# A two-layer hybrid encoder on one core: q and k prepared for two token tiles at a time, large products taken off GpSimd, and the last steps of A's second unit moved behind the gate of C

## The chip, the cores and the metric

The kernel runs on one core of a Trainium2 chip. The number that counts is the device time in microseconds. The engines are TensorE (PE, with its weight load PEld), VectorE (DVE), ScalarE (ACT), GpSimd (POOL) and SyncE (SP, which here issues every DMA).

## The reference, cut to what matters

The input is 512 tokens of 1024 channels. Two layers follow each other; every layer normalises x, modulates it (scale, shift and gate come from a conditioning vector), multiplies it with one wide `w_in`, runs three mixers, multiplies their joined outputs with `w_out` and adds the gated result to x.

```python
for l in range(DEPTH):                                   # 2 layers
    shift, scale, gate = jnp.split(cs @ w_ada[l] + b_ada[l], 3, axis=-1)
    h = rms_norm(x, norm_g[l]) * (1.0 + scale[:, None]) + shift[:, None]
    qa, ka, va, ga, qb, kb, vb, gb, qc, kc, vc, gc = jnp.split(h @ w_in[l], split_idx, axis=-1)
    qa = rope(rms_norm(qa, qn_a[l]), ROT_THETA, ROT_A)   # A: 4 heads, two 32-wide maps each
    ka = rope(rms_norm(ka, kn_a[l]), ROT_THETA, ROT_A)
    oa = diff_attention(qa, ka, va, lam, ...)            # softmax1 - lam * softmax2, then rms_norm
    oa = oa * jax.nn.silu(ga)
    qb, kb = (rope(rms_norm(z, g), ROT_THETA, ROT_B) for z, g in ((qb, qn_b[l]), (kb, kn_b[l])))
    ob = dilated_attention(qb, kb, vb) * jax.nn.silu(gb) # B: 6 heads of 64
    qc, kc = (rope(z, RET_THETA, DK_C) for z in (qc, kc))
    oc = retention_bidir(qc, kc, vc, ret_decay[l], gn_c[l]) * jax.nn.silu(gc)   # C: 4 heads
    x = x + gate[:, None] * (jnp.concatenate([oa, ob, oc], axis=-1) @ w_out[l])
```

## The kernel before, in words

Tokens stand in four tiles of 128 (`NT`). Every weight is split into a rounded high part and a rest (`whi`, `wlo`), and so is the activation (`hT`, `hL`), so that each product of a layer is three matmuls (`products`, lines 342 to 348). The split costs ACT one copy (line 156) and DVE one subtraction (line 315) per piece of weights.

The columns of `w_in` come in chunks. Their order in a layer is: C's q, k and v; A's unit 0; B's unit 0; A's unit 1; B's units 1 and 2; the gate of C; the gate of B; then the output projection in two halves. Each chunk is 16 groups of matmuls (4 pieces of weights by 4 token tiles; the gate of B has 12). Everything that is not a product is hung on a plan: `at(g, fn)` runs `fn` right after group `g` is emitted, so the numbers at the top of the file say behind which group a step is written. A scheduler then sorts the instructions of each engine; each engine executes its own list strictly in that order. PE's list therefore holds, between the products of the next chunks, the attention work of the units before: scores (`sc`), transpositions (`tr`, four at a time, `tr4`, line 572, into a single buffer), values (`pv`).

What the change touches:

- `Unit`: a unit is two heads of q and k. `done` (per token tile) copies the tile's 256 columns of q and k from the accumulator to `qkraw` (a pool of four buffers). `norm` squares them on ACT into `qkn`, sums on DVE (line 625), finishes the mean on DVE (line 587) and takes the power -0.5 on POOL (line 199); it turns the rotary columns with two products and a sum (lines 633, 634, 635, all on DVE). `scale` multiplies by the result on POOL (line 639). `turn` transposes a pair of tiles on PE and writes the high and the low part (`nat`, ACT and DVE at line 159 for the low part); `stack` moves them with DMAs.
- `Attention.turn`: transposes the exponentials (`e` of A, `sb` of B) and copies them out of the transposition buffer on ACT or DVE (`pt`, line 708). `values` is the product with v.
- `Diff.finish` to `finish4`: the end of an A unit. `finish` copies the sums (`oat`); `finish2` transposes them, copies them (`oao`), squares them on POOL (`oasq`, line 765), sums (line 769); `finish3` scales (line 779) and multiplies by the gate on POOL (line 781); `finish4` transposes back and splits into `o`. `FIN2, FIN3, FIN4 = 4, 12, 16` say how many groups after the end of the attention they are written, for both units.
- `Retention.rope` (C's q and k): two products and a sum, of which two are on POOL (lines 913, 916). `Retention.gate_done` (lines 988 to 992) applies C's gate: `cth`, which also frees the accumulator bank. There are four banks.
- `out_done`: the residual sum is on POOL for the first half of the columns (line 1134).
- `Dilated.soft`: one reciprocal per head (line 813).

Buffers: `ep` is a ring of five tiles of 512 columns, tag `e`, from which scores, exponentials and many temporaries of all units come.

Of the kernel before, what the change touches and what calls it, by code (L numbers as in the profile page):

```python
# [48 lines left out]
E_T1, E_T2, E_X, E_QF, E_SCALE_A, E_SCALE_B = 1, 1, 1, 0, 0, 0  # L49
FIN2, FIN3, FIN4 = 4, 12, 16  # L50
# [84 lines left out]
def encoder(ctx, tc, x, c, norm_g, w_ada, b_ada, w_in, w_out, params, consts, out):  # L135
# [5 lines left out]
    four = pool("four", 4)  # L141
# [448 lines left out]
    class Unit:  # L590
# [6 lines left out]
        def done(self, t, ps, g0):  # L597
# [20 lines left out]
        def norm(self, t):  # L618
            n, ng_ = self.n, 256 // self.n
            rot, h = n // 4, n // 8  # L620
            raw = self.raw[t]
            qn = self.qn[t] = two.tile([P, ng_, n], F32, name="qkn", tag=f"qkn{t % 2}")
            act(qn.rearrange("p g n -> p (g n)"), raw, AF.Square)
            ss = self.ss[t] = sm.tile([P, 8], F32, name="qkss")[:, :ng_]
# [691 lines left out]
```

## Time and profile before

| | |
|---|---|
| time, three runs | 649.25, 651.51, 651.46 us, median 651.46 us |
| the profiled execution | 650.6 us, of which the span from first to last instruction is 648.7 us |
| PE busy | 622.2 us of the span |
| DVE busy | 491.8 us |
| ACT busy | 344.4 us |
| POOL busy | 163.7 us |

How to read it: busy is the union of an engine's instructions, so a PE that is busy nearly always leaves only the rest of the span to be won without changing the products. A line number belongs to the file before. In a group of instructions the mean is of one instruction; in a timeline an idle time in brackets stands before the instruction and names what ended it. Idle marks of PE are a little short, because a matmul's end is modelled and reaches beyond the start of the next one; the distance from start to start shows more.

### The profile page before, as it was taken

To read this page: it belongs to the slowest core of one execution; us is meant where nothing else is said; L and a number is where in the kernel's file an instruction comes from. 1 tells how busy PE (TensorE), PEld (TensorE's weight loads), DVE (VectorE), ACT (ScalarE), POOL (GpSimd) and SP (SyncE) were. 2 spreads that over 40 slices of the span, in tenths; PEclk is the share of its full clock that TensorE was granted. 3 is DMA by queue.
4 is the path that set the end of the run, shared out by engine and by line. 5 is a ranking of instruction groups with operands and counts; after the bars stand their busy time and mean duration, and the time that the engine had idled before them with its cause. 6 is when DMAs were issued, how large, how long until landed. Compare 5 with 4: busy or idle time off the path is not lost.

```text
span 648.7 us, 10469 instructions
## 1 busy us (share of the span) xinstructions
PE 622.2 (96%) x3487; PEld 512.2 (79%) x3487; DVE 491.8 (76%) x1206; ACT 344.4 (53%) x756; POOL 163.7 (25%) x183
## 2 busy tenths in 40 slices
PE   6899999999999996999999999999999999899997
PEld 1788888987888873677779998997788787677786
DVE  4787676689988987898969364768997997578443
ACT  4855263566646665564424344455756577566410
POOL 1105452514350510200411041633323340020000
PEclk9799999999999999999999999999999999999999
DMA  8998123535555556476643322235565453604211
GB/s 302 295 293 238 55 70 98 135 98 146 150 152 176 141 176 161 160 248 201 216 156 110 90 73 66 71 104 159 134 176 137 135 145 112 161 34 149 80 65 66
DMA packets 87277, 93.03 MB, mean 143 GB/s; under 512 B 7188, under 2 KB 68276, under 8 KB 87224
## 3 DMA queue, kind: packets, MB, share of 16 engines
q1 hardware_dynamic: 87224, 92.37, 48.0%
q8 instruction: 28, 0.46, 0.3%
q14 instruction: 25, 0.20, 0.1%
HBM read 72.42 MB, written 4.19 MB: 118 GB/s over the span
## 4 chain that ended last, share of the span: by engine, by line
PE 79%; DVE 9%; issue 4%; DMA 3%; POOL 3%; ACT 2%; SPq 1%; POOLq 0%; ACTq 0%
PE acc L346 16%; PE acc L348 16%; PE acc L347 16%; PE tr L572 8%; PE pv L718 5%; PE sc L741 2%; DMA x<-in_x_dram 2%; PE acc L344 1%; PE acc L342 1%; PE acc L343 1%; PE sc L802 1%; PE sc L803 1%; DVE wlo L315 1%; PE co L971 1%; DVE pt L708 1%
## 5 line engine op out<-in xcount | busy, mean ns | idle before, releaser
L346 PE MATMUL acc<-whi,hT 128*128 128x384 f32 (+1 forms) x424 | 154.7, 365 | 0.0
L347 PE MATMUL acc<-wlo,hT 128*128 128x384 f32 (+1 forms) x424 | 151.8, 358 | 0.0
L348 PE MATMUL acc<-whi,hL 128*128 128x384 f32 (+1 forms) x424 | 151.8, 358 | 0.0
L315 DVE TENSOR_TENSOR wlo<-raw,whi 128x384 fp32r<-128x384 f32 (+1 forms) x130 | 80.7, 650 | 26.7 <-ACT whi L156 26.4
L199 POOL TENSOR_TENSOR qkss<-qkss,nhalf 128x4 f32<-128x4 f32 (+1 forms) x40 | 52.6, 1315 | 128.3 <-DVE qkss L587 127.3
L346 PEld LDWEIGHTS acc<-whi,hT 128*128 128x128 f32 x424 | 80.0, 189 | 6.1
L348 PEld LDWEIGHTS acc<-whi,hL 128*128 128x128 f32 x424 | 79.8, 188 | 6.2
L347 PEld LDWEIGHTS acc<-wlo,hT 128*128 128x128 f32 x424 | 80.0, 189 | 5.5
L156 ACT ACTIVATE whi<-raw 128x768 fp32r<-128x768 f32 (+2 forms) x67 | 59.5, 890 | 39.7 <-PE acc L348 33.8
L159 DVE SCALAR_TENSOR_TENSOR ada_acc<-raw,cs,ada_acc 128x512 f32<-128x512 f32 x86 | 64.3, 749 | 3.9 <-DMA raw<-in_w_ada_dram 3.3
L156 ACT ACTIVATE e<-sc,mx 128x512 f32<-128x512 f32 x64 | 43.9, 689 | 35.5 <-DVE mx L743 16.9
L743 DVE TENSOR_REDUCE mx<-sc 128x1 f32<-128x512 f32 x64 | 43.5, 685 | 9.5 <-PE sc L741 8.8
L156 ACT ACTIVATE sb<-sb,mx 128x512 f32<-128x512 f32 x48 | 34.4, 717 | 20.4 <-DVE mx L807 20.2
L718 PE MATMUL pv<-pt,v 128*64 128x256 f32 x320 | 38.9, 385 | 1.0 <-DVE pt L708 0.9
L156 ACT ACTIVATE pt<-tr 128x512 f32<-128x512 f32 x40 | 23.8, 596 | 23.1 <-PE tr L572 22.9
L572 PE MATMUL tr<-cst,sb 128*128 128x128 f32 x192 | 30.7, 283 | 5.3 <-DVE nat L159 2.2
L807 DVE CUSTOM_DVE_ANT_0 sb<-sc,cst 128x512 f32<-128x512 f32 x48 | 32.1, 683 | 4.4 <-PE sc L803 2.6
L572 PEld LDWEIGHTS tr<-cst,sb 128*128 128x128 f32 x192 | 21.9, 142 | 16.0 <-ACT pt L156 7.7
L718 PEld LDWEIGHTS pv<-pt,v 128*64 128x64 f32 x320 | 21.2, 136 | 16.2 <-DVE pt L708 5.5
L708 DVE COPY pt<-tr 128x512 f32<-128x512 f32 x40 | 27.4, 684 | 7.8 <-PE tr L572 7.8
L639 POOL TENSOR_TENSOR qkn<-qkraw,qkss 128x256 f32<-128x256 f32 x40 | 30.0, 751 | 5.9 <-DVE qkraw L635 2.0
L741 PE MATMUL sc<-stk,stq 96*128 96x512 f32 x64 | 27.3, 434 | 1.0 <-ACT e L156 0.9
(294 smaller groups left out, 1367.8 us busy)
## 6 DMA issues: line engine op xcount, KB each, us to landing
raw<-in_w_ada_dram SPq DMA_DIRECT2D x64, 256.0 KB, 3.2
raw<-in_w_in_dram SPq DMA_DIRECT2D x48, 192.0 KB, 2.9
raw<-in_w_in_dram SPq DMA_DIRECT2D x24, 384.0 KB, 3.4
raw<-in_w_in_dram SPq DMA_DIRECT2D x32, 256.0 KB, 3.4
raw<-in_w_ada_dram SPq DMA_DIRECT2D x16, 512.0 KB, 5.1
raw<-in_w_out_dram SPq DMA_DIRECT2D x32, 256.0 KB, 3.0
x<-in_x_dram SPq DMA_DIRECT2D x8, 512.0 KB, 4.2
stB<-nat SPq DMA_DIRECT2D x32, 128.0 KB, 2.4
```

The source lines that it names most:

```text
L156: A.activation(o, i, f, **kw)
L159: V.scalar_tensor_tensor(o, a, s, b, op0, op1)
L199: G.tensor_tensor(o, i, nhalf[:, :n], OP.pow)
L315: V.tensor_tensor(l2[:, z], r2[:, z], h2[:, z].bitcast(F32), OP.subtract)
L346: T.matmul(ps, ah, hi[i], start=s_, stop=False)
L347: T.matmul(ps, ah, lo[i], start=False, stop=False)
L348: T.matmul(ps, al, hi[i], start=False, stop=e_)
L572: T.transpose(ps[:, i, :], b, ident)
L708: V.tensor_copy(pt, ps)
L718: T.matmul(self.pv[h * 64:h * 64 + 64, i * 256:i * 256 + 256], self.u.v[:, k, h * 64:h * 64 + 64], self.pt[h][:, k], start=k == 0, stop=k ...
L741: T.matmul(ps, self.u.stq[0:96, m, tok_(qt)], self.u.stk[0:96, m], start=True, stop=True)
L743: V.tensor_reduce(mx, ps, AX.X, OP.max, negate=True)
```

## The change

Four things are changed.

1. `norm` and `scale` work on a pair of token tiles (512 columns) instead of one (256). Each is called half as often, behind the second tile of the pair. `scale` is on DVE and is held in program order there. The pool `four` is gone: `qkraw` is now two buffers of a pair, and the gain loads `ng` and the tiles `hn` share the new sizes.
2. No large product is left on POOL: `scale`, the square of `finish2` (now on ACT), the gate product of `finish3`, two of the three steps of C's rotary turn and the residual sum of the first half are moved to DVE or ACT. POOL keeps the powers, the memsets and the rotary tables.
3. `FIN_A = (4, 12, 16), (14, 6, 9)`: unit 0 of A ends as before (4, then 12 and 16 after the first); unit 1 starts its `finish2` at 14 instead of 4, `finish3` at 20 instead of 16 and `finish4` at 23 instead of 20. `oat` and `oao` no longer take tiles of the ring `e`; they use the tiles in which the unit's output will stand, and `out_pair` is called in `finish4`.
4. `soft` takes one reciprocal for both heads.

```diff
-E_T1, E_T2, E_X, E_QF, E_SCALE_A, E_SCALE_B = 1, 1, 1, 0, 0, 0
-FIN2, FIN3, FIN4 = 4, 12, 16
+FIN_A = (4, 12, 16), (14, 6, 9)
-    four = pool("four", 4)
-        g = four.tile([P, 256], F32, name="ng", tag="qkraw")
+        g = two.tile([P, 256], F32, name="ng", tag="qkraw")
...
             g = g0 + 12 + t
-            at(g + NORM, self.norm, t)
-            at(g + SCALE, self.scale, t)
             if t % 2:
+                at(g + NORM, self.norm, t // 2)
+                at(g + SCALE, self.scale, t // 2)
                 at(g + TURN, self.turn, t // 2)
...
-        def norm(self, t):
-            n, ng_ = self.n, 256 // self.n
+        def norm(self, i):
+            n, ng_ = self.n, 512 // self.n
-            raw = self.raw[t]
-            qn = self.qn[t] = two.tile([P, ng_, n], F32, name="qkn", tag=f"qkn{t % 2}")
-            act(qn.rearrange("p g n -> p (g n)"), raw, AF.Square)
-            ss = self.ss[t] = sm.tile([P, 8], F32, name="qkss")[:, :ng_]
+            raw = self.raw[i].rearrange("p t (g n) -> p (t g) n", n=n)
+            qn = self.qn[i] = two.tile([P, ng_, n], F32, name="qkn")
+            act(qn, raw, AF.Square)
+            ss = self.ss[i] = sm.tile([P, 16], F32, name="qkss")[:, :ng_]
             V.tensor_reduce(ss, qn, AX.X, OP.add)
             rms_end(ss, ng_, n)
...
-        def scale(self, t):
-            n, ng_ = self.n, 256 // self.n
-            (V if (E_SCALE_A if n == DK_A else E_SCALE_B) % 2 else G).tensor_tensor(self.qn[t], self.raw[t].rearrange("p (g n) -> p g n", n=n),
-                            self.ss[t].unsqueeze(2).to_broadcast([P, ng_, n]), OP.mult)
+        def scale(self, i):
+            n, ng_ = self.n, 512 // self.n
+            tc.keep_in_program_order(V.tensor_tensor(self.qn[i], self.raw[i].rearrange("p t (g n) -> p (t g) n", n=n),
+                                                     self.ss[i].unsqueeze(2).to_broadcast([P, ng_, n]), OP.mult))
...
         def finish(self, g):
-            self.ob = ep.tile([P, S], F32, name="oat", tag="e")
+            self.ob = one.tile([P, S], F32, name="oat", tag=f"s{2 * self.k + 1}")
             act(self.ob, self.pv)
-            at(g + FIN2, self.finish2, g + FIN2)
+            at(g + self.fin[0], self.finish2, g + self.fin[0])
...
-            G.tensor_tensor(sq, o, o, OP.mult)
+            act(sq, o, AF.Square)
...
-            at(g + FIN3, self.finish3)
-            at(g + FIN4, self.finish4)
+            at(g + self.fin[1], self.finish3)
+            at(g + self.fin[2], self.finish4)
...
-            G.tensor_tensor(on, on, self.u.ga, OP.mult)
+            V.tensor_tensor(on, on, self.u.ga, OP.mult)
...
-            split(self.oh, self.ol, ps.rearrange("p t m -> p (t m)"))
+            split(*self.out_pair(self.k), ps.rearrange("p t m -> p (t m)"))
...
+            V.reciprocal(self.s, self.s)
             for h in range(2):
-                V.reciprocal(self.s[h], self.s[h])
...
-            G.tensor_tensor(t1.rearrange("p h (w n) -> p h w n", w=2), sw,
+            V.tensor_tensor(t1.rearrange("p h (w n) -> p h w n", w=2), sw,
...
-            G.tensor_tensor(self.qkp[:, :, :DK_C], raw, t1, OP.add)
+            V.tensor_tensor(self.qkp[:, :, :DK_C], raw, t1, OP.add)
...
-                    (V if hf * E_X % 2 else G).tensor_tensor(x_sb[t][:, cols], y, x_sb[t][:, cols], OP.add)
+                    V.tensor_tensor(x_sb[t][:, cols], y, x_sb[t][:, cols], OP.add)
```

How the instructions stand, at three places. In these rows a name carries its buffer's number; line numbers of the new file are two to six lower than those of the old one.

First place: PE in layer 0, where the products of C's gate have ended and those of B's gate (lines 342 to 344 before, 340 to 342 after) begin. `sb` are exponentials of B's units, `oat` the sums of A's unit 1. Before:

```order
L572 MATMUL tr_3033<-cst_103,sb_2932 128x128 x4
L802 MATMUL sc_3139<-stk_2907,stq_2906 128x512
L803 MATMUL sc_3139<-stk_2907,stq_2906 128x512
L572 MATMUL tr_3040<-cst_103,sb_2940 128x128 x4
L572 MATMUL tr_3047<-cst_103,oat_2926 128x128 x4
L572 MATMUL tr_3102<-cst_103,sb_2994 128x128 x4
L342 MATMUL acc_3175<-hT_118,whi_2977 128x512
L343 MATMUL acc_3175<-hL_119,whi_2977 128x512
L572 MATMUL tr_3108<-cst_103,sb_3002 128x128 x4
L344 MATMUL acc_3175<-hT_118,wlo_2978 128x512
L342 MATMUL acc_3175<-hT_118,whi_2977 128x512
L343 MATMUL acc_3175<-hL_119,whi_2977 128x512
```

After:

```order
L570 MATMUL tr_2882<-cst_100,sb_2786 128x128 x4
L800 MATMUL sc_2972<-stk_2760,stq_2759 128x512
L801 MATMUL sc_2972<-stk_2760,stq_2759 128x512
L340 MATMUL acc_3005<-hT_115,whi_2828 128x512
L341 MATMUL acc_3005<-hL_116,whi_2828 128x512
L570 MATMUL tr_2889<-cst_100,sb_2793 128x128 x4
L342 MATMUL acc_3005<-hT_115,wlo_2829 128x512
L340 MATMUL acc_3005<-hT_115,whi_2828 128x512
L341 MATMUL acc_3005<-hL_116,whi_2828 128x512
L342 MATMUL acc_3005<-hT_115,wlo_2829 128x512
L340 MATMUL acc_3038<-hT_115,whi_2828 128x512
L341 MATMUL acc_3038<-hL_116,whi_2828 128x512
```

The four transpositions of `oat` have left this place (they stand some 70 rows later, between products of B's gate), and the products of B's gate begin two transpositions earlier and stand between the others.

Second place: PE in layer 1, a little earlier in the layer, behind the second pair of q and k of B's unit 2 (`qkn`). Before, from the pair's last transposition on:

```order
L572 MATMUL tr_6424<-cst_103,qkn_6296 128x128
L347 MATMUL acc_6307<-wlo_6389,hT_118 128x384
L802 MATMUL sc_6512<-stB_6016,stC_6015 128x512
L803 MATMUL sc_6512<-stB_6016,stC_6015 128x512
L348 MATMUL acc_6307<-whi_6388,hL_119 128x384
L346 MATMUL acc_6333<-whi_6388,hT_118 128x384
L347 MATMUL acc_6333<-wlo_6389,hT_118 128x384
L348 MATMUL acc_6333<-whi_6388,hL_119 128x384
L346 MATMUL acc_6333<-whi_6388,hT_118 128x384
L347 MATMUL acc_6333<-wlo_6389,hT_118 128x384
```

After, from the transposition ahead of it to the next two:

```order
L570 MATMUL tr_6099<-cst_100,sb_5985 128x128 x4
L800 MATMUL sc_6202<-stB_5735,stC_5734 128x512
L801 MATMUL sc_6202<-stB_5735,stC_5734 128x512
L570 MATMUL tr_6115<-cst_100,qkn_5991 128x128 x4
L800 MATMUL sc_6209<-stB_5735,stC_5734 128x512
L801 MATMUL sc_6209<-stB_5735,stC_5734 128x512
L570 MATMUL tr_6170<-cst_100,sb_6060 128x128 x4
L570 MATMUL tr_6176<-cst_100,sb_6067 128x128 x4
```

Before, products stood between that pair and the next transposition (five more follow the rows shown); now a pair of score products is all that stands on either side of it.

Third place: DVE in the same stretch of layer 1, the work around the low parts `nat` of that pair. Before:

```order
L708 COPY pt_6413<-tr_6408 128x4x128
L807 ISA sb_6467,mx_6466<-sc_6463,cst_103 128x512
L807 ISA mx_6466 128x1
L813 RECIPROCAL bs_6461<-bs_6461 128x1
L159 SCALAR_TENSOR_TENSOR nat01_6349<-tr_6424,gcol_115,nat00_6348 128x256
L813 RECIPROCAL bs_6469<-bs_6469 128x1
L818 TENSOR_SCALAR sb_6467<-sb_6467,bs_6469 128x512
L159 SCALAR_TENSOR_TENSOR nat11_6351<-tr_6424,gcol_115,nat10_6350 128x256
L807 ISA sb_6516,mx_6515<-sc_6512,cst_103 128x512
L807 ISA mx_6515 128x1
L708 COPY pt_6413<-tr_6487 128x4x128
```

After:

```order
L705 COPY pt_6104<-tr_6099 128x4x128
L636 TENSOR_TENSOR qkn_5991<-qkraw_5934,qkss_5993 128x512
L809 RECIPROCAL bs_6146<-bs_6146 128x2
L805 ISA sb_6206,mx_6205<-sc_6202,cst_100 128x512
L805 ISA mx_6205 128x1
L815 TENSOR_SCALAR sb_6158<-sb_6158,bs_6146 128x512
L313 TENSOR_TENSOR wlo_6304<-raw_6259,whi_6303 128x384
L157 SCALAR_TENSOR_TENSOR nat01_6043<-tr_6115,gcol_112,nat00_6042 128x256
L313 TENSOR_TENSOR wlo_6304<-raw_6259,whi_6303 128x384
L157 SCALAR_TENSOR_TENSOR nat11_6045<-tr_6115,gcol_112,nat10_6044 128x256
```

The scaling of the pair (`qkn`) now stands in DVE's list between a copy `pt` and the low parts; before it was no instruction of DVE.

## Rows read from the trace of the kernel before

**Rows 1.** The page, part 1: busy time, share of the span and instructions of each engine.

```profile
PE 622.2 (96%) x3487; PEld 512.2 (79%) x3487; DVE 491.8 (76%) x1206; ACT 344.4 (53%) x756; POOL 163.7 (25%) x183
```

**Rows 2.** The span in stages (stretch in us, its length, busy us and instructions of PE, PEld, DVE, ACT, POOL, the granted TensorE clock, DMA share, GB/s). The first stage up to 60 us, the start, is not among them. 140 to 244 and 430 to 556 are the attention of layers 0 and 1, 244 to 263 and 556 to 569 the end of C's gate in them, 100 to 140 and 263 to 430 what lies between.

```profile
100.00:140.00 40.00, 38.79 (x236) 34.72 (x235) 28.35 (x68) 18.80 (x41) 13.46 (x13) 1.00 0.44 123
140.00:244.00 104.00, 101.21 (x603) 84.36 (x602) 94.88 (x242) 67.61 (x168) 35.05 (x45) 1.00 0.53 147
244.00:263.00 19.00, 13.30 (x71) 8.43 (x70) 14.55 (x36) 10.01 (x21) 1.51 (x2) 0.91 0.72 185
263.00:430.00 167.00, 166.01 (x924) 141.26 (x923) 124.08 (x270) 75.54 (x148) 39.76 (x38) 1.00 0.42 135
430.00:556.00 126.00, 125.11 (x716) 103.25 (x715) 108.05 (x285) 81.27 (x201) 36.43 (x36) 1.00 0.49 137
556.00:569.00 13.00, 10.27 (x65) 6.93 (x64) 7.54 (x20) 8.14 (x17) 1.04 (x1) 1.00 0.73 184
```

**Rows 3.** Timeline of PE, layer 0, end of C's gate: start in us, duration in us, instruction, in brackets the idle time before it and what ended it.

```profile
255.17 0.40 PE L803 MATMUL sc<-stk,stq 128*128 128x512 f32 x1
255.78 0.65 PE L572 MATMUL tr<-cst,sb 128*128 128x128 f32 x4 [0.22 <-ACT pt L156]
257.22 0.66 PE L572 MATMUL tr<-cst,oat 128*128 128x128 f32 x4 [0.78 <-DVE pt L708]
258.57 0.84 PE L572 MATMUL tr<-cst,sb 128*128 128x128 f32 x4 [0.69 <-ACT oao L156]
259.54 0.79 PE L342 MATMUL acc<-hT,whi 128*128 128x512 f32 x1
260.13 0.63 PE L343 MATMUL acc<-hL,whi 128*128 128x512 f32 x1
...
261.87 0.60 PE L342 MATMUL acc<-hT,whi 128*128 128x512 f32 x1
262.30 0.42 PE L343 MATMUL acc<-hL,whi 128*128 128x512 f32 x1
262.55 0.39 PE L344 MATMUL acc<-hT,wlo 128*128 128x512 f32 x1
```

**Rows 4.** The same of layer 1.

```profile
563.89 0.66 PE L572 MATMUL tr<-cst,sb 128*128 128x128 f32 x4 [0.22 <-ACT pt L156]
565.33 0.65 PE L572 MATMUL tr<-cst,oat 128*128 128x128 f32 x4 [0.79 <-DVE pt L708]
566.67 0.66 PE L572 MATMUL tr<-cst,sb 128*128 128x128 f32 x4 [0.69 <-ACT oao L156]
567.64 0.50 PE L342 MATMUL acc<-hT,whi 128*128 128x512 f32 x1 [0.31 <-DVE cth L159]
```

**Rows 5.** Timeline of PE, layer 0: the second pair of q and k of B's unit 2 and the transposition behind it.

```profile
246.25 0.63 PE L572 MATMUL tr<-cst,qkn 128*128 128x128 f32 x4 [0.40 <-DVE pt L708]
...
249.72 0.63 PE L572 MATMUL tr<-cst,sb 128*128 128x128 f32 x4 [2.22 <-DVE nat L159]
```

**Rows 6.** Timeline of POOL in layer 0, same columns.

```profile
181.55 1.04 POOL L199 TENSOR_TENSOR qkss<-qkss,nhalf 128x4 f32<-128x4 f32 x1 [11.93 <-DVE qkss L587]
182.67 0.61 POOL L639 TENSOR_TENSOR qkn<-qkraw,qkss 128x256 f32<-128x256 f32 x1
...
191.28 1.53 POOL L781 TENSOR_TENSOR oao<-oao,ga 128x512 f32<-128x512 f32 x1 [1.01 <-DVE oao L779]
```

**Rows 7.** Timeline of DVE in the same time.

```profile
181.98 0.21 DVE L635 TENSOR_TENSOR qkraw<-rt,rt 128x64 f32<-128x64 f32 x1
...
182.78 0.58 DVE L635 TENSOR_TENSOR qkraw<-rt,rt 128x64 f32<-128x64 f32 x1
...
191.12 2.11 DVE L315 TENSOR_TENSOR wlo<-raw,whi 128x384 fp32r<-128x384 f32 x2
```

**Rows 8.** Groups of DVE's instructions by line and shape over the whole span: times, busy us, mean ns of one, idle us before them.

```profile
L315 DVE TENSOR_TENSOR wlo<-raw,whi 128x384 fp32r<-128x384 f32 x90 | 50.5, 589 | 14.2 <-ACT whi L156 14.0
L743 DVE TENSOR_REDUCE mx<-sc 128x1 f32<-128x512 f32 x64 | 43.5, 685 | 9.5 <-PE sc L741 8.8
L315 DVE TENSOR_TENSOR wlo<-raw,whi 128x512 fp32r<-128x512 f32 x40 | 30.2, 788 | 12.5 <-ACT whi L156 12.5
L635 DVE TENSOR_TENSOR qkraw<-rt,rt 128x64 f32<-128x64 f32 x40 | 11.3, 282 | 0.1
L625 DVE TENSOR_REDUCE qkss<-qkn 128x4 f32<-128x256 f32 x24 | 9.8, 407 | 0.0
L813 DVE RECIPROCAL bs<-bs 128x1 f32<-128x1 f32 x48 | 7.5, 157 | 5.5 <-ACT sb L156 5.3
...
L159 DVE SCALAR_TENSOR_TENSOR ga<-th,acc 128x128 f32<-128x128 f32 x16 | 4.5, 280 | 0.1
...
L992 DVE TENSOR_TENSOR cno<-cno,cth 128x384 f32<-128x384 f32 x8 | 4.4, 548 | 0.0
...
L779 DVE TENSOR_TENSOR oao<-oao,oass 128x512 f32<-128x512 f32 x4 | 2.8, 689 | 0.1
```

**Rows 9.** The same of POOL.

```profile
L639 POOL TENSOR_TENSOR qkn<-qkraw,qkss 128x256 f32<-128x256 f32 x40 | 30.0, 751 | 5.9 <-DVE qkraw L635 2.0 <-DVE oass L770 1.0 <-POOL qkss L199 0.2
L199 POOL TENSOR_TENSOR qkss<-qkss,nhalf 128x8 f32<-128x8 f32 x16 | 27.5, 1718 | 48.7 <-DVE qkss L587 48.6
L199 POOL TENSOR_TENSOR qkss<-qkss,nhalf 128x4 f32<-128x4 f32 x24 | 25.1, 1046 | 79.6 <-DVE qkss L587 78.7 <-ACT v L156 0.9
```

More of the change, by code (lines that the diff above doesn't have):

```diff
@@ L577, in split, with h_tile @@
         V.tensor_tensor(lo, src, hi.bitcast(F32), OP.subtract)
-    def h_tile(t, q, rstd):
+    def h_tile(hn, t, q, rstd):
         f = slice(q * 256, q * 256 + 256)
-        hn = two.tile([P, 256], F32, name="hn", tag=f"qkn{q % 2}")
         stt(hn, x_sb[t][:, f], rstd[t], mods[q][:, 256:], OP.mult, OP.mult)
         V.tensor_tensor(hn, hn, mods[q][:, :256], OP.add)
-        return hn
     def rms_end(s, n, width):
@@ L601, in done @@
                     self.ga = two.tile([P, NT, P], F32, name="ga")
-            n, ng_ = self.n, 256 // self.n
-            raw = self.raw[t] = four.tile([P, 256], F32, name="qkraw")
-            act(raw, ps[:, 0:256])
+            if t % 2 == 0:
+                self.raw[t // 2] = two.tile([P, 2, 256], F32, name="qkraw")
+            act(self.raw[t // 2][:, t % 2], ps[:, 0:256])
             act(self.v[:, t], ps[:, 256:384])
@@ L644, in turn @@
                 self.nat = [[one.tile([P, S], F32R, name=f"nat{w}{z}", tag=f"nat{2 * w + z}") for z in range(2)] for w in range(2)]
-            q2 = [self.qn[2 * i + j].rearrange("p g n -> p (g n)") for j in range(2)]
-            ps = tr4([q2[j][:, w * P:(w + 1) * P] for w in range(2) for j in range(2)])
+            q2 = self.qn[i].rearrange("p (t g) n -> p t (g n)", t=2)
+            ps = tr4([q2[:, j, w * P:(w + 1) * P] for w in range(2) for j in range(2)])
             o = slice(2 * i * P, (2 * i + 2) * P)
@@ L721, in encoder, with __init__ @@
     class Diff(Attention):
-        def __init__(self, unit, g0, gap, oh, ol):
-            self.oh, self.ol = oh, ol
+        def __init__(self, unit, g0, gap, fin, k, out_pair):
+            self.k, self.out_pair, self.fin = k, out_pair, fin
             self.m = {}
@@ L755, in finish @@
         def finish(self, g):
-            self.ob = ep.tile([P, S], F32, name="oat", tag="e")
+            self.ob = one.tile([P, S], F32, name="oat", tag=f"s{2 * self.k + 1}")
             act(self.ob, self.pv)
-            at(g + FIN2, self.finish2, g + FIN2)
+            at(g + self.fin[0], self.finish2, g + self.fin[0])
         def finish2(self, g):
             ps = tr4([self.ob[:, tok_(t)] for t in range(NT)])
-            o = self.o = ep.tile([P, 8, DV_A], F32, name="oao", tag="e")
+            o = self.o = one.tile([P, 8, DV_A], F32, name="oao", tag=f"s{2 * self.k}")
             act(o.rearrange("p g d -> p (g d)"), ps.rearrange("p t m -> p (t m)"))
             sq = ep.tile([P, 8, DV_A], F32, name="oasq", tag="e")
-            G.tensor_tensor(sq, o, o, OP.mult)
+            act(sq, o, AF.Square)
             ss = self.ss = sm.tile([P, 8], F32, name="oass")
@@ L931, in turn_f @@
         def turn_f(self, t):
-            (V.tensor_copy if E_QF % 2 else act)(self.qfT[:, :, tok_(t)], tr4([self.fq[:, h] for h in range(4)]))
+            act(self.qfT[:, :, tok_(t)], tr4([self.fq[:, h] for h in range(4)]))
         def state(self, t):
@@ L1104, in h_all @@
         def h_all(t, q):
-            hn = [h_tile(t, q + j, rstd_next) for j in range(2)]
-            ps = tr4([hn[j][:, k * P:(k + 1) * P] for j in range(2) for k in range(2)])
+            hn = two.tile([P, 2, 256], F32, name="hn", tag="qkn")
+            for j in range(2):
+                h_tile(hn[:, j], t, q + j, rstd_next)
+            ps = tr4([hn[:, j, k * P:(k + 1) * P] for j in range(2) for k in range(2)])
             split(hT[:, 2 * q:2 * q + 4, tok_(t)], hL[:, 2 * q:2 * q + 4, tok_(t)], ps)
```

23 lines of the change are left out of this document (10 added, 13 removed).

## The prediction

> **What bounds the kernel now.** The page's busy times come first: PE is busy for 622.2 us of a span of 648.7 [rows 1], and the change removes no matmul. What can be won is therefore only PE's idle time, 26.5 us in all, and of that only what follows the start. The stages tell where it lies [rows 2]: subtract PE's busy time from each stage's length. The two ends of C's gate, 244 to 263 and 556 to 569, hold 5.7 and 2.7 us of it in 32 us. The attention of layer 0 (140 to 244) holds 2.8, that of layer 1 (430 to 556) 0.9, and the two stretches between hold 1.2 and 1.0, together 5.9. The remaining 12 us lie in the start up to 60 us, whose instructions stand in the same order as before, and in the last drain. So the change is worth what it does at the two ends of the gate, plus a share of 5.9.
>
> In the stage 244 to 263 the reader should see that PE and DVE are both far from full while the transpositions go one after the other: each waits for the copy that empties the one buffer, [0.78 <-DVE pt], [0.69 <-ACT oao] [rows 3]. In 140 to 244, DVE is busy for 94.9 of 104 us [rows 2], the next nearest limit.
>
> **Part 1, unit 1's end moved behind the gate of C.** In layer 0 PE goes from the score product at 255.17 to the first product of B's gate at 259.54 [rows 3]; between them stand three groups of transpositions and, ahead of them, one product. The idle marks of that piece add to 0.22 + 0.78 + 0.69 = 1.7 us. The distances say more, because a group of four transpositions needs far less than the 1.35 us from the `oat` group to the next: if 0.4 us is taken for a group (an estimate, below the 0.65 of its row, whose modelled end reaches too far) and 0.25 for the product, 4.37 - 0.25 - 3 x 0.4 = 2.9. In the new order no group stands between, and the transpositions of `sb` come among the products, which are their cover. So the gain is 1.7 to 2.9; I take 2.3. The first place of the order bears this out as far as position goes; it also needs C's gate (`cth`) to have freed a bank by then, which ACT did behind `oao`, and `oao` is gone from there. The four `oat` transpositions still cost their own columns later, hidden by nothing, but they cost these before too.
>
> In layer 1 the same piece has idle marks of 0.22 + 0.79 + 0.69 + 0.31 = 2.0 us [rows 4], by distance 2.9 as before. I take 2.4.
>
> There is one more item in layer 0. Behind the idle stretch the products start 0.59 (259.54 to 260.13) and 0.43 us (261.87 to 262.30) apart, and at the end of these rows 0.25 [rows 3]; the stage's granted clock is 0.91, where the other five stages show 1.00 [rows 2], so part of it ran at 1.2 instead of 2.4 GHz. Five such steps at about 0.28 too much make 1.4 us. Layer 1 had 2.7 us idle in 13 and kept 1.00. With layer 0's idle time only shortened I take half, 0.7, between 0 and 1.4.
>
> Steps behind it: `finish4` of unit 1 now ends some 37 products of 512 columns ahead of the first use of its output (counted in the order); at 0.24 us that is over 8 us for one copy and one subtraction of 0.69 [rows 8], so nothing is late. If that cover were missing it would cost about 2 us per layer. The ring `e` gets two tiles back for that time, which can only shorten waits and which I cost at nothing.
>
> **Part 2, pairs and no products on GpSimd: what DVE pays.** Added to DVE: 20 scalings of 512 columns at 0.689, the product of the same shape (line 779) [rows 8], = 13.8; four gate products and four residual sums at 0.689 = 5.5; 16 steps of C's turn at 0.548 = 8.8. Together 28.1. Removed: 40 sums of 256 at 0.407 become 20 of 512 at 0.685, minus 2.6; the 20 means and 24 reciprocals that disappear, at 0.157, minus 6.9; 120 small products of 64 columns become 60 of 128: at an undisturbed 0.21 [rows 7] against 0.28 (the 128-column row), minus 25.2 + 16.8 = 8.4. Net 28.1 - 17.9 = +10.2 us.
>
> Against that stands what POOL's products take from DVE now. The sum `qkraw` took 0.21 beside a power and 0.58 beside the scaling `qkn` [rows 6, 7]; two subtractions took 2.11 us beside the gate product `oao` of 1.53 [rows 6, 7], where two undisturbed ones of that width would be 1.1 (0.548 each [rows 8]). Over the span this shows in the means: 90 subtractions of 384 at 0.589 instead of 0.548 (3.7), 40 of 512 at 0.788 instead of 0.689 (4.0), 40 sums at 0.282 instead of 0.21 (2.9): 10.6 us in three groups alone, and other two-input groups add to it. So DVE's load stays about the same or falls by some us, and the 30 us of `qkn` on POOL [rows 9] leave the chain.
>
> The Trainium skill ("SBUF — State Buffer", section "Who interferes with whom") says that a DVE instruction with two SBUF inputs contends with a GpSimd instruction that reads SBUF, and that the second one blocks until the first finishes. The rows agree for the large products and differ for the powers, which also read SBUF and beside which `qkraw` kept its 0.21. By the rule, the powers would hold DVE as well, 16 x 1.718 + 24 x 1.046 = 52.6 us of them before; afterwards, at my estimate of 3.1 for 16 columns, 8 x 3.1 + 12 x 1.718 = 45.4, so a further 7 us would be freed, which leans to the larger gain below.
>
> What is this worth to PE? Nothing, if its 5.9 us of idle time outside the gates end on ACT or on the one transposition buffer; 5.9 at most. New waits could also come, up to 2 us. I take 3, half of the most, because DVE is at 91% in the stage that holds half of it and at 86% in layer 1 [rows 2].
>
> **Part 3, the scaling in DVE's list.** This costs. `scale` used to be done ahead by POOL; now it stands behind whatever DVE has in front of it, and PE's transposition of the pair waits for it. In layer 0 that transposition already waited [0.40 <-DVE pt] [rows 5]; now 0.69 of scaling follows that same copy: +0.7 (0 to 1). The next transposition waits 2.22 for the low parts as before. In layer 1 the second place of the order puts the same pattern where products stood: before, there was no such wait; now the rows of layer 0 are its price, 0.40 + 0.69 + 2.22 = 3.3, less something for a DVE list that lacks layer 0's sums of the modulation: +3.0 (1.5 to 3.5).
>
> Waits on POOL: the power of 16 columns is not in the trace; from 4 to 8 columns it grows by 0.67 [rows 9], so 16 would be 3.1, an estimate, against two of 1.72 in a row before. The scaling waits for it in DVE's list, and everything behind it there waits too. In the order the pairs' scalings stand far enough behind their means (at least some 3 us of DVE work in the places I counted), so I cost it at nothing; without that cover it is 1 to 3 us for each pair. SP: the gain loads `ng` now share two buffers instead of four and stand apart in SP's list; behind each stand weights of the output and of the next layer, ordered several us ahead. Nothing, or up to 1 us.
>
> **Sum.** -2.3 - 2.4 - 0.7 - 3.0 + 0.7 + 3.0 = -4.7 us against the profiled execution of 650.6 us: 645.9. The median of the three runs is 0.9 above that execution, so I forecast 646.8. Its own range, from the bounds of the single terms added with some mutual compensation, is 642 to 651.
>
> **Rivals.** (a) No change to speak of. The transposition buffer and ACT, not DVE, end the scattered waits, so part 2 gives nothing and the clock item neither; and layer 1's new wait comes in full: -2.3 - 2.4 + 1.0 + 3.5 = -0.2, that is 651.3. For it: all of rows 3's marks are copies out of that buffer. Against: DVE makes about half of those copies.
> (b) A larger gain. DVE's freed time reaches PE everywhere, the clock stays up, and the layer 1 wait is small: -2.9 - 2.9 - 1.4 - 5.9 + 0.7 + 1.5 = -10.9, that is 640.6. For it: DVE at 91%. Against: PE loses only 5.9 outside the gates by its own marks.
> (c) Slower. The in-order scaling makes DVE stand for POOL's power: 8 pairs of A at 1.5 us and 12 of B at 0.9 make 23, of which PE's products cover perhaps half: +11 on the forecast, 657.8. It decides where less than about 3 us of DVE work lies between the mean and the scaling. Against it speaks the order, for it that POOL's queue also carries the rotary tables.
>
> **Chances.** Forecast 0.48, (a) 0.24, (b) 0.16, (c) 0.12. A measurement of this kernel can tell about 0.5% from no change, 3.3 us: faster means below 648.2, slower above 654.7. Of the forecast some 0.36 lie below 648.2 and 0.12 within; (a) gives 0.03 to faster, 0.19 to no change, 0.02 to slower; (b) is all faster; (c) is slower. So 0.55, 0.31, 0.14. The range that leaves out 2 in 10 is 640 to 655.
>
> **What would show it.** Right: no idle mark with `oao` in front of B's gate products in either layer, a granted clock nearer 1.00 in layer 0's gate stage, means of 0.55 and 0.69 for the subtractions, and a new wait for `nat` in layer 1 near 556. Wrong: idle time of DVE before `qkn` released by POOL (then (c)); PE's idle time in 140 to 244 as before although the means fell (then (a)).

## The result and the profile after

The changed kernel takes 656.59 us in the median of 7 runs (653.42 to 657.28), the kernel before 650.53 (649.25 to 652.21): a ratio of 1.0076, with a 95% interval of 1.0051 to 1.0100. It is slower by 0.8%, and the time lies above the range that was given. The profiled execution took 657.28 us, its span is 655.3.

The page after, part 1, against [rows 1]:

```profile
PE 627.0 (96%) x3487; PEld 514.5 (79%) x3487; DVE 489.3 (75%) x1126; ACT 345.8 (53%) x740; POOL 90.9 (14%) x95
```

POOL lost 73 us of work and DVE's total fell by 2.5, within what the prediction gave ("about the same or falls by some us"). But PE, with the same 3487 matmuls, is busy 4.8 us longer. The stages show where, same columns as [rows 2]:

```profile
140.00:244.00 104.00, 101.42 (x590) 83.20 (x589) 89.79 (x208) 67.27 (x162) 22.52 (x25) 0.98 0.49 135
244.00:263.00 19.00, 14.46 (x73) 9.80 (x72) 16.68 (x37) 10.20 (x21) 0.00 (x0) 0.82 0.74 198
430.00:556.00 126.00, 124.68 (x712) 104.06 (x711) 105.06 (x241) 80.14 (x192) 18.96 (x10) 1.00 0.49 139
556.00:569.00 13.00, 8.37 (x43) 5.32 (x43) 8.60 (x21) 7.47 (x15) 0.00 (x0) 0.79 0.46 103
```

Before, the granted clock was 0.91 and 1.00 at the two ends of the gate [rows 2]; now it is 0.82 and 0.79, and 0.98 in layer 0's attention. Finer windows of the same view find three stretches at 1.2 GHz (0.50) between the start and the last drain:

```profile
209.00:211.00 2.00, 2.00 (x12) 1.08 (x10) 2.00 (x5) 0.00 (x0) 0.00 (x0) 0.50 0.08 25
...
253.00:259.00 6.00, 4.53 (x22) 2.59 (x22) 5.34 (x12) 3.12 (x6) 0.00 (x0) 0.50 0.82 183
...
564.00:570.00 6.00, 4.53 (x21) 2.43 (x20) 3.89 (x9) 3.11 (x6) 0.00 (x0) 0.50 0.88 199
```

The kernel before has one, by the same view half as long:

```profile
259.00:262.00 3.00, 2.87 (x11) 1.88 (x10) 2.57 (x7) 1.38 (x3) 0.63 (x1) 0.50 0.89 251
```

What PE did before the last of them stands in its timeline, layer 1:

```profile
557.16 0.42 PE L346 MATMUL acc<-whi,hL 128*128 128x384 f32 x1
558.10 0.66 PE L570 MATMUL tr<-cst,sb 128*128 128x128 f32 x4 [0.52 <-ACT pt L154]
...
560.22 0.63 PE L570 MATMUL tr<-cst,qkn 128*128 128x128 f32 x4 [1.00 <-DVE bs L809]
...
563.18 0.88 PE L570 MATMUL tr<-cst,sb 128*128 128x128 f32 x4 [1.65 <-DVE nat L157]
564.75 1.11 PE L570 MATMUL tr<-cst,sb 128*128 128x128 f32 x4 [0.69 <-ACT pt L154]
566.64 3.68 PE L715 MATMUL pv<-pt,v 128*64 128x256 f32 x16 [0.78 <-DVE pt L705]
570.26 0.66 PE L570 MATMUL tr<-cst,sb 128*128 128x128 f32 x4
```

557.16 is the last gate-in product (`acc`). From there PE has only transpositions and four score products, and waits 0.52 + 1.00 + 1.65 + 0.69 + 0.78 = 4.6 us, five times in a row. The mark with `bs` is the wait for the scaling: the inferred releaser is one instruction off, as DVE's timeline at the same place of layer 0 shows, where PE's transposition starts at 249.49:

```profile
248.66 0.68 DVE L636 TENSOR_TENSOR qkn<-qkraw,qkss 128x512 f32<-128x512 f32 x1
249.26 0.15 DVE L809 RECIPROCAL bs<-bs 128x2 f32<-128x2 f32 x1
```

Behind the waits the 16 products of the values take 3.68 us; at the full clock they take 1.95 (below). Layer 0 has the same picture from 249.49 to 259.76. The `oat` and `oao` marks of [rows 3, 4] are gone, as forecast.

Groups of DVE and POOL by line and shape (columns as in [rows 8, 9]):

```profile
L313 DVE TENSOR_TENSOR wlo<-raw,whi 128x384 fp32r<-128x384 f32 x90 | 47.4, 553 | 13.6 <-ACT whi L154 13.6
L313 DVE TENSOR_TENSOR wlo<-raw,whi 128x512 fp32r<-128x512 f32 x40 | 26.3, 689 | 12.5 <-ACT whi L154 12.5
L636 DVE TENSOR_TENSOR qkn<-qkraw,qkss 128x512 f32<-128x512 f32 x20 | 13.7, 687 | 0.0
...
L197 POOL TENSOR_TENSOR qkss<-qkss,nhalf 128x16 f32<-128x16 f32 x8 | 24.4, 3052 | 131.3 <-DVE qkss L583 131.3
L197 POOL TENSOR_TENSOR qkss<-qkss,nhalf 128x8 f32<-128x8 f32 x12 | 20.9, 1745 | 107.4 <-DVE qkss L583 107.4
```

The subtractions fell to 553 and 689 ns, the power of 16 columns takes 3.05 us, and DVE was idle 0.0 us ahead of its 20 scalings: it does not stand for POOL's power, so rival (c), which gave nearly this time, is not what happened.

### The profile page after: what moved, and what is told of

The parts are those of the page before. It is cut to its first block, busy times and chain, and to the rows that moved or that the text cites. A ratio compares the mean times of both kernels' runs of the same rounds, so it can differ in the third digit from the quotient of the medians.

```text
span 655.3 us, 10177 instructions
## 1 busy us (share of the span) xinstructions
PE 627.0 (96%) x3487; PEld 514.5 (79%) x3487; DVE 489.3 (75%) x1126; ACT 345.8 (53%) x740; POOL 90.9 (14%) x95
## 4 chain that ended last, share of the span: by engine, by line
PE 81%; issue 10%; DVE 4%; ACT 2%; DMA 1%; SPq 1%; POOL 0%; POOLq 0%; ACTq 0%; DVEq 0%
PE acc L344 18%; PE acc L346 17%; PE acc L345 17%; PE tr L570 8%; PE pv L715 5%; PE sc L738 3%; DMA raw<-in_w_ada_dram 1%; PE sc L800 1%; PE sc L801 1%; PE co L968 1%; PE kv L935 1%; PE co L967 1%; PE line L527 1%; PE acc L342 1%; PE ada_ps L477 1%
## 5 line engine op out<-in xcount | busy, mean ns | idle before, releaser
L313 DVE TENSOR_TENSOR wlo<-raw,whi 128x384 fp32r<-128x384 f32 (+1 forms) x130 | 73.7, 595 | 26.1 <-ACT whi L154 26.0
L197 POOL TENSOR_TENSOR qkss<-qkss,nhalf 128x8 f32<-128x8 f32 (+1 forms) x20 | 45.4, 2268 | 238.6 <-DVE qkss L583 238.6
L715 PE MATMUL pv<-pt,v 128*64 128x256 f32 x320 | 44.0, 423 | 3.8 <-DVE pt L705 3.8
L715 PEld LDWEIGHTS pv<-pt,v 128*64 128x64 f32 x320 | 23.2, 149 | 20.8 <-DVE pt L705 7.8
L738 PE MATMUL sc<-stk,stq 96*128 96x512 f32 x64 | 28.1, 443 | 1.9 <-ACT e L154 1.9
L154 ACT ACTIVATE nat<-tr,gcol 128x256 fp32r<-128x256 f32 x40 | 18.8, 470 | 11.7 <-PE tr L570 8.0
```

Of the source, the lines that this page charges most:

```text
L154: A.activation(o, i, f, **kw)
L197: G.tensor_tensor(o, i, nhalf[:, :n], OP.pow)
L313: V.tensor_tensor(l2[:, z], r2[:, z], h2[:, z].bitcast(F32), OP.subtract)
L715: T.matmul(self.pv[h * 64:h * 64 + 64, i * 256:i * 256 + 256], self.u.v[:, k, h * 64:h * 64 + 64], self.pt[h][:, k], start=k == 0, stop=k ...
L738: T.matmul(ps, self.u.stq[0:96, m, tok_(qt)], self.u.stk[0:96, m], start=True, stop=True)
```

## Experiments

The labels T and R1 to R6 stand for the theories that the runs were to tell apart. Theory T: the loss sits where the last pair of unit B2 is turned after the gate-in products have run out; the waits then stand in a row and the clock falls behind them. Rivals: R1, DVE held in order has too much in its list; R2, the moved end of unit 1 costs; R3, R5, the pairs, or the work moved to DVE, cost by themselves; R4, R6, that an earlier turn only shifts the waits, or helps by its due time alone; and that the slow clock is only a mark beside the loss. Ratios are against the kernel before, with 95% intervals; 0.01 is 6.5 us. The kernel before was measured again beside each group of runs (medians of 650.43 to 651.69 us), so runs of different groups are compared by their ratios and not by their times.

### The parts, one by one

**fin_alone**: the kernel before with the move alone.

```diff
-FIN2, FIN3, FIN4 = 4, 12, 16
+FIN_A = (4, 12, 16), (14, 6, 9)
```

> The kernel before with only the move of unit 1's end behind the gate of C; single tiles, products and scalings on GpSimd as before. T: layer 1's second pair keeps its products, and both ends of the gate lose the waits for the copies of the unit's end, 2 to 2.5 us each, so 645 to 648; a slow clock may stay in layer 0's end (1 to 2 us, then up to 649). R1: the same, 645 to 648. R2: 652 to 656.

644.34 us, ratio 0.9889 (0.9874 to 0.9905), a little under T's range. R2 falls: the move gains 1.1%. Layer 1's end (556 to 569) has no wait and no slow clock left; layer 0's keeps its waits, and its slow clock lasts longer than before the change (0.82 against 0.91), as the stages show, and below them the 16 products there in PE's timeline:

```profile
244.00:263.00 19.00, 15.61 (x82) 10.46 (x82) 16.17 (x37) 9.07 (x20) 0.00 (x0) 0.82 0.80 216
...
556.00:569.00 13.00, 13.00 (x84) 9.32 (x84) 9.87 (x24) 7.64 (x15) 0.00 (x0) 1.00 0.55 148
```

```profile
249.07 3.68 PE L718 MATMUL pv<-pt,v 128*64 128x256 f32 x16 [0.78 <-DVE pt L708]
```

**fin_undone**: the changed kernel without the move, `FIN_A = (4, 12, 16), (4, 12, 16)`.

> The changed kernel with unit 1's end put back in front of the gate of C; pairs and scaling on DVE as in the change. Its order keeps the second pair of layer 1 without products around it and brings the groups of the unit's end back between it and B's gate products. T: all waits of the changed kernel stay and the two ends get 2 to 2.5 us each back, so 659 to 662. R1: as T, 659 to 662. R2: back to the time before, 650 to 652.

664.58 us, ratio 1.0184 (1.0154 to 1.0214), above what any theory said; by its ratio, with the kernel before at 650.53 as when the ranges were set, it is 662.5, just above T's. Inside the change the move is worth 1.0184 - 1.0076 = 1.1%, as alone.

**fin_nopool**: fin_alone with the large products off GpSimd; single tiles, scaling left there.

```diff
-            G.tensor_tensor(sq, o, o, OP.mult)
+            act(sq, o, AF.Square)
-            G.tensor_tensor(on, on, self.u.ga, OP.mult)
+            V.tensor_tensor(on, on, self.u.ga, OP.mult)
...
```

> The kernel before with the move of unit 1's end and with the large products off GpSimd (square on ACT, the rest on DVE), but single tiles and the scaling still on GpSimd. Its order keeps layer 1's products around the last tiles. T (the places of the turns decide, not GpSimd's contention with DVE): 642 to 647, about the 644.3 of the move alone. By the prediction's second part (relief of DVE reaches PE): 640 to 642. Rival R3 (products on DVE cost PE more than the contention did): 648 or more.

640.53 us, ratio 0.9848 (0.9833 to 0.9863): 0.4%, 2.7 us, under the move alone. That is the size that the prediction's second part gave it; my T gave it nothing. DVE's busy time is as before (492.1 us against 492.3 in fin_alone), since the products now stand in its own list. Three waits of fin_alone behind the gate of layer 0, which neither the kernel before nor fin_nopool has at these instructions, are gone:

```profile
278.75 0.50 PE L802 MATMUL sc<-stk,stq 128*128 128x512 f32 x1 [0.82 <-DVE mx L807]
...
289.01 0.66 PE L572 MATMUL tr<-cst,sb 128*128 128x128 f32 x4 [0.58 <-ACT pt L156]
...
291.53 0.63 PE L572 MATMUL tr<-cst,oao 128*128 128x128 f32 x4 [0.47 <-DVE pt L708]
```

**scale_pool**: the changed kernel, the pair's scaling on GpSimd.

```diff
-            tc.keep_in_program_order(V.tensor_tensor(self.qn[i], ...))
+            G.tensor_tensor(self.qn[i], ...)
```

> The changed kernel with the pair's scaling back on GpSimd; pairs, products off GpSimd and the move stay. In its order the last pair has products in front of it in both layers. T: layer 1's gate end costs nothing and layer 0's less, so 646 to 650. Rival R5 (it is the pairs as such, which come as late as their second tile, wherever they are scaled): 653 to 658, with new waits of PE for the pair, now ended by GpSimd.

645.07 us, ratio 0.9918 (0.9904 to 0.9932), by 1 us better than T had it, and R5's 653 to 658 falls. Against fin_nopool, which differs by the pairs (with their two large buffers in place of four, and the single reciprocal of `soft`), it is 0.7% slower.

**nopool_single**: the kernel before with the products and the scaling off GpSimd, single tiles, no move.

> The kernel before with the large products and the scalings taken off GpSimd (square on ACT, the rest on DVE) but single token tiles and the unit's end where it was. In its order layer 1's second pair has lost its products, as in the changed kernel. T: DVE's relief from GpSimd is worth 0 to 3 us and layer 1's end costs 5 to 7, so 652 to 657. Rival R3 (it is the pairs that cost, by the doubled power on GpSimd and longer instructions on DVE): without pairs 645 to 650.

655.57 us, ratio 1.0058 (1.0045 to 1.0071). A loss comes without pairs too, and as in the changed kernel, layer 1's order has no products left around the last turn. If the parts add, the scaling on DVE costs 1.0% here (0.6% lost although the products off GpSimd are worth 0.4%), and 1.6% with pairs, held in order (1.0076 - 0.9918). So R3 falls as the main cause, but the pairs are not free: fin_undone, which like this run is without the move and has them, is 1.0184 - 1.0058 = 1.3% slower. scale_pool shows 0.7% of that with the scaling on GpSimd; the rest, which pairs share with the held scaling, is not separated.

### The place

**scale_free**: the changed kernel, the scaling on DVE but free to be placed.

> The changed kernel, with the pair's scaling still on DVE but free for the scheduler to place, not held in program order. In its order layer 1's second pair of unit B2 has gate-in products around it again (as before the change), layer 0's end of the gate is as in the changed kernel. Theory T (the loss is the second pair of layer 1 being turned when no products are left, so that the waits for its scaling, its low part and the copies stand in a row and the granted clock falls behind them): the wait of 1.16 for the pair and the slow clock near 566 go, about 6 us, so 648 to 652. Rival R1 (DVE in its fixed order stands for GpSimd's power in many places, or DVE simply has too much to do): the scaling is still on DVE, so 654 to 657. Rival R2 (the move of the unit's end behind the gate costs by itself): 655 to 657, since the move is still in.

657.36 us, ratio 1.0095 (1.0080 to 1.0110): T's number missed by 5 us, and by the time alone R1 and R2, whose ranges end at 657, fit better. Layer 1's end is mended (the clock from 556 to 569 is 1.00), but the free scaling opened one wait elsewhere, in front of a pair of layer 0; the line below it is DVE's, a little earlier:

```profile
106.69 1.09 PE L570 MATMUL tr<-cst,qkn 128*128 128x128 f32 x4 [4.66 <-DVE nat L157]
```

```profile
100.50 0.69 DVE L636 TENSOR_TENSOR qkn<-qkraw,qkss 128x512 f32<-128x512 f32 x1 [2.70 <-POOL qkss L197]
```

Here DVE does stand for POOL's power, 2.7 us: the mechanism of the prediction's rival (c), which the changed kernel does not show (0.0). So the time does not tell for or against T; R2 falls with fin_alone, R1 with turn_5. It does show what holding the scaling in order was good for.

**turn_5**: everything of the change, scaling still held in DVE's order, one step earlier.

```diff
-NORM, SCALE, TURN, STACK = 1, 5, 6, 6
+NORM, SCALE, TURN, STACK = 1, 4, 5, 5
```

> The changed kernel with everything in it, the scaling held in DVE's order too; only scaling, transposition and stacking of a pair are due one step earlier. In its order layer 1's last pair has gate-in products before and behind it again; layer 0's end is as in the changed kernel. Theory T (the loss sits where the last pair of unit B2 is turned with no products left: its waits stand in a row and the granted clock falls behind them): layer 1 loses the waits and the slow clock of its gate end, 4 to 6 us, so 651 to 653. Rival R1 (DVE, held in order, stands for GpSimd's power): with the scaling due earlier it stands longer, so 657 to 661.

646.19 us, ratio 0.9929 (0.9915 to 0.9944): 1.5% under the changed kernel, more than T asked for, and R1 falls, since DVE's list holds the same work. Between the same instructions layer 1 is 5.9 us shorter, which is what T asked for (4 to 6); 4.4 more are won in layer 0, though its gate end still has a clock of 0.82 (the table below has both). Its stage there, and its timeline of PE at layer 1's end:

```profile
244.00:263.00 19.00, 15.29 (x81) 10.16 (x81) 16.21 (x35) 9.60 (x21) 0.00 (x0) 0.82 0.85 241
```

```profile
552.23 0.60 PE L570 MATMUL tr<-cst,qkn 128*128 128x128 f32 x4
...
553.76 0.34 PE L346 MATMUL acc<-whi,hL 128*128 128x384 f32 x1
555.07 0.63 PE L570 MATMUL tr<-cst,sb 128*128 128x128 f32 x4 [0.96 <-DVE nat L157]
556.38 0.66 PE L570 MATMUL tr<-cst,sb 128*128 128x128 f32 x4 [0.69 <-ACT pt L154]
557.82 1.95 PE L715 MATMUL pv<-pt,v 128*64 128x256 f32 x16 [0.78 <-DVE pt L705]
```

With products before and behind the pair the wait for it is gone, that for `nat` is 0.96 instead of 1.65, and the 16 products take 1.95.

**turn_5_b2**: the same step for unit B2 only, after which the order at layer 1's end is still without products.

> The changed kernel with scaling, transposition and stacking due one step earlier for unit B2 alone. In its order the last pair of layer 1 still has no products around it. T: the row of waits and the slow clock at the ends of the gate stay, so 654 to 658. Rival R6 (what helped before was that the last pair's own scaling was due earlier): as with all units, 645 to 649.

654.74 us, ratio 1.0059 (1.0042 to 1.0076). The gate end is as bad as in the changed kernel: PE waits only 0.31 instead of 1.00 for the pair, but 2.17 instead of 1.65 behind it. R6 falls: an earlier due time of that pair alone does not help. In all runs of the changed kernel's family the loss at layer 1's end goes with the missing products.

```profile
556.00:569.00 13.00, 9.05 (x42) 5.37 (x42) 7.68 (x20) 6.98 (x16) 0.00 (x0) 0.75 0.63 148
```

**turn_4**: two steps earlier, `1, 3, 4, 4`.

> The changed kernel with scaling, transposition and stacking due two steps earlier in all units. Layer 1's last pair has many products around it, layer 0's last has six in front and none behind. T: at or under the 646.2 of one step, 640 to 647. R1 (DVE, held in order, stands for GpSimd's power of 16 columns, the more the earlier the scaling): 648 to 656.

641.96 us, ratio 0.9855 (0.9835 to 0.9874), as T had it.

### The clock by itself

**warm**: the changed kernel, every engine's order kept, with PE given work in one wait of each layer.

```diff
+                for _ in range(7 if self.warm and qt == NT - 1 and h else 0):
+                    T.matmul(ps, self.u.stq[:, h, tok_(qt)], self.u.stk[:, h], start=True, stop=True)
                 T.matmul(ps, self.u.stq[:, h, tok_(qt)], self.u.stk[:, h], start=True, stop=False)
```

> The changed kernel, every engine's order the same, but the first product of one score of unit B1 (last token tile, second head) is done eight times instead of once, so that TensorE has 7 x 0.234 = 1.6 us of work in the wait for the low parts of the last pair (1.87 us in layer 0, 1.65 in layer 1). Same output. If the wait makes the granted clock fall (theory T): the slow stretches from 253 and 563 on shorten or go, which gives back up to 3.5 us in each layer, less some delay of that score: 650 to 655, with the 16 products of the values there near 1.9 us instead of 3.6. If the clock falls for another reason, or its fall costs nothing on the path: 656.6 to 660, and the values stay at 3.6 us.

651.02 us, ratio 0.9999 (0.9983 to 1.0016): 0.8% under the changed kernel, though PE does 14 products more. Its timeline of PE in layer 1:

```profile
555.79 0.63 PE L570 MATMUL tr<-cst,qkn 128*128 128x128 f32 x4 [1.00 <-DVE bs L811]
556.37 1.90 PE L801 MATMUL sc<-stB,stC 128*128 128x512 f32 x7
...
558.76 0.63 PE L570 MATMUL tr<-cst,sb 128*128 128x128 f32 x4
560.07 0.66 PE L570 MATMUL tr<-cst,sb 128*128 128x128 f32 x4 [0.69 <-ACT pt L154]
561.51 1.95 PE L715 MATMUL pv<-pt,v 128*64 128x256 f32 x16 [0.78 <-DVE pt L705]
```

The other waits stand as they were (1.00, 0.69, 0.78), and from the pair to the next transposition it is 558.76 - 555.79 = 2.97 us, against 563.18 - 560.22 = 2.96: the chain is no shorter, only the wait for `nat` is filled. Yet the same 16 products take 1.95 instead of 3.68 us. In its stages the clock at both ends of the gate is 1.00:

```profile
244.00:263.00 19.00, 16.07 (x96) 11.39 (x96) 18.96 (x42) 11.09 (x24) 0.00 (x0) 1.00 0.80 215
...
556.00:569.00 13.00, 11.50 (x70) 8.21 (x68) 9.29 (x22) 7.87 (x17) 0.00 (x0) 1.00 0.66 164
```

So the wait is what makes the clock fall at these two places, and the fall costs time on the path: about 0.8% of the kernel, half of it in each layer (the table below).

### Together

**fin_turn4**: fin_alone with `1, 3, 4, 4`.

> The kernel before with only the move of unit 1's end, and with scaling, transposition and stacking due two steps earlier (single tiles, scaling on GpSimd as before). In its order the last tiles of B2 have products around them in layer 0 too. T: the row of waits at layer 0's gate end and the slow clock from 247 on go, 3 to 5 us under the 644.3 of the move alone, so 639 to 642. Rival R4 (the waits only change their place: GpSimd's scaling is not done by then, or the stack's transfers land no earlier): 643.5 to 647.

637.61 us, ratio 0.9807 (0.9791 to 0.9823), 1.4 us under T's range; R4 falls. Layer 0's end has its products back, at a clock of 1.00:

```profile
244.00:263.00 19.00, 18.82 (x109) 13.26 (x110) 18.54 (x44) 11.67 (x27) 0.53 (x1) 1.00 0.82 234
```

**fin_nopool_t4**: fin_nopool with `1, 3, 4, 4`.

> The kernel before with the move of unit 1's end, the large products off GpSimd (single tiles, scaling left on GpSimd) and the turns two steps earlier: the parts that gained, together. If they add: 637.6 less the 3.8 that the products gave beside the move, 632 to 636. If the relief of DVE is worth less once the turns have their cover: 636 to 639.

635.94 us, ratio 0.9771 (0.9753 to 0.9789), the fastest version: 2.3% under the kernel before, 3.0% under the changed one. Taking the products off GpSimd adds 0.4%, as without the earlier turns.

## Why the prediction was wrong, step by step

The chain before, fin_alone, fin_nopool, scale_pool, changed kernel adds the four parts in turn. The bullets give differences of ratios, times 650.5 us. The table gives, for the profiled executions, the time in us between the starts of the same four products of PE; in the changed kernel they are these:

```profile
28.10 0.39 PE L344 MATMUL acc<-stq,hT 128*128 128x512 f32 x1
...
260.72 0.39 PE L340 MATMUL acc<-hT,whi 128*128 128x512 f32 x1
...
343.19 0.34 PE L344 MATMUL acc<-wsp,hT 128*128 128x384 f32 x1
...
570.99 0.39 PE L340 MATMUL acc<-hT,whi 128*128 128x512 f32 x1
```

| | before | fin_alone | fin_nopool | scale_pool | changed | turn_5 | warm |
|---|---|---|---|---|---|---|---|
| start to the first product | 27.4 | 26.5 | 27.1 | 27.1 | 28.1 | 27.2 | 26.5 |
| layer 0, to B's gate | 232.1 | 227.8 | 228.0 | 228.0 | 232.6 | 228.2 | 230.1 |
| from there to layer 1 | 82.9 | 84.7 | 82.1 | 83.6 | 82.5 | 83.4 | 82.1 |
| layer 1, to B's gate | 225.2 | 219.7 | 219.1 | 221.6 | 227.8 | 221.9 | 225.4 |
| from there to the end | 81.1 | 83.2 | 82.7 | 84.0 | 84.3 | 84.0 | 84.2 |

- **Part 1, the move**: -2.3 - 2.4 - 0.7 = -5.4 forecast, -7.2 measured (-1.1% alone and in the change). Right in kind, too small by a quarter. Its clock item went the other way: layer 0's slow stretch did not shrink but doubled, from 0.91 to 0.82 in its stage of fin_alone.
- **Part 2, products off GpSimd**: -3.0 forecast, 0.9848 - 0.9889 = -2.7 measured. The size is right, the place is not, so the size owes something to luck: 2.6 us of the gain lie between B's gate of layer 0 and layer 1, where the prediction counted 1.0 us of idle time and where the three waits shown for fin_alone had opened behind the move. The means of the subtractions came out at the figures named. By the rule of the Trainium skill that was weighed there ("SBUF — State Buffer", section "Who interferes with whom") the powers should block such subtractions too; 45.3 us of powers of q and k are left on POOL (24.4 for 16 columns, 12 x 1.745 for 8), and the means, 553 and 689 ns, are within 5 ns of the undisturbed durations in [rows 8]. Taken one by one, 16 of the 130 subtractions of the changed kernel ran beside a power; they took 550 and 688 ns, those beside nothing on POOL 550 and 685. The measurement decides against the rule for these powers.
- **Part 2, pairs**: costed at nothing beyond DVE's columns. 0.9918 - 0.9848 = +4.6 measured, with the scaling on GpSimd. By the table 2.5 us of it lie in layer 1 up to B's gate and the rest in the two stretches behind the gates; what causes it I did not separate.
- **Part 3, the scaling in DVE's list**: +0.7 and +3.0 = 3.7 forecast, 1.0076 - 0.9918 = +10.3 measured. By the table 4.6 us of it lie in layer 0 and 6.1 in layer 1, both ahead of B's gate.

The step that failed is part 3's price. For layer 1 it was "now the rows of layer 0 are its price, 0.40 + 0.69 + 2.22", taken as 3.0; 6.1 was measured. The pattern was foreseen, the wait came where it was put, and the two waits of the pair, 1.00 and 1.65, are no longer than priced. What the price left out is the clock: it was treated as something the change could only give back ("with layer 0's idle time only shortened I take half"), while layer 1 "kept 1.00". With the new row of waits it fell there, and warm, which leaves every other instruction in its place, gets 227.8 - 225.4 = 2.4 us back in layer 1. warm wins as much at layer 0's gate end, but that half is not part 3's: fin_alone has the same clock of 0.82 there.

For layer 0 the price was +0.7, at the gate's end, and 4.6 was measured, most of it earlier, at a place that the prediction does not name. There PE has no product for 9.7 us, from 204.71 to 214.39:

```profile
204.71 0.34 PE L346 MATMUL acc<-whi,hL 128*128 128x384 f32 x1
...
206.47 0.66 PE L570 MATMUL tr<-cst,sb 128*128 128x128 f32 x4 [0.98 <-ACT pt L154]
...
208.42 3.62 PE L715 MATMUL pv<-pt,v 128*64 128x256 f32 x16
...
213.49 0.50 PE L738 MATMUL sc<-stk,stq 96*128 96x512 f32 x1 [0.87 <-ACT e L154]
...
214.39 0.43 PE L344 MATMUL acc<-whi,hT 128*128 128x384 f32 x1
```

No pair is turned here, so T, which speaks of the last pair of unit B2, is too narrow: it is again a stretch of PE's list without products, with waits (for ACT) and the clock at 0.50 from 209 to 211. In scale_pool and turn_5 products stand in this stretch, and no wait over 0.4 us. turn_5, with the scaling still in DVE's list, is within 0.3 us of scale_pool in every row of the table. So part 3's loss is that of the order, in both layers, and not of DVE's load. With that one line of numbers the change runs at 646.2; that this is next to the 646.8 of the forecast is luck, since the move gained more and the pairs cost more than was put down.

Rival (c) had nearly the right time for the wrong reason: DVE did not wait for the power (idle 0.0 ahead of the scalings). Rival (a) had layer 1's wait at 3.5, still short of the 6.1, and part 2 at nothing, which was worth 2.7 us.

Open: why some orders with the scaling on DVE use up the products ahead of that turn (the changed kernel, turn_5_b2, nopool_single) and others do not (turn_5, scale_free). Also open is what in a row of waits makes the clock fall. Before the change layer 0 had a row much like that of layer 1 now, 0.17 + 0.40 + 2.22 + 0.69 + 0.39 = 3.9 us ([rows 5] and the lines below), and the 16 products behind it still took 1.95; the clock fell only from 259 on, after three more waits [rows 3].

```profile
244.72 0.66 PE L572 MATMUL tr<-cst,sb 128*128 128x128 f32 x4 [0.17 <-ACT pt L156]
...
251.04 0.66 PE L572 MATMUL tr<-cst,sb 128*128 128x128 f32 x4 [0.69 <-ACT pt L156]
...
252.56 1.95 PE L718 MATMUL pv<-pt,v 128*64 128x256 f32 x16 [0.39 <-DVE pt L708]
```

## What to carry to other kernels

When a step moves from one engine's list to another, look at what stands around its consumer on the bottleneck engine: with products around it PE waited 0.96 us behind the turn of layer 1's last pair (turn_5); without them the same stretch of the kernel cost 6 us more, and a second stretch without products 4 us. Price a row of waits on TensorE with what the clock does behind it, not only with the sum of its idle marks. And take a change apart before judging it: here one part was worth 1.1%, one 0.4%, the pairs lost 0.7%, and the 1.6% that the scaling on DVE lost was nearly undone by moving three due times one step.

## What the runs showed of the hardware

Giving TensorE 1.6 us of useless products in one wait of each layer made the kernel 5 us faster: the granted clock stayed at 2.4 GHz at both ends of the gate (1.00 instead of 0.82 and 0.79). The Trainium skill ("TensorE: Matmul & The Clock Gate", section "HAM oscillation — how this bites in real kernels") tells of a matmul kernel whose waits for DMA bring the lower clock back; the rows here agree, with waits for copies out of the transposition buffer in their place. A power on POOL grows with its columns: 1.05 us for 4 [rows 9], 1.75 for 8, 3.05 for 16, so that a pair of A's tiles (3.05) saves little against two single ones of 1.72 [rows 9].
